# Layer 0 pooling: DMAs from SyncE to ScalarE, and a piece spread over three hooks

## The chip, the cores and the metric

The kernel runs on one core of one Trainium2 chip, in one launch. The metric is the device time of one execution in microseconds; lower is better. TensorE (PE) does the matmuls, VectorE (DVE), ScalarE (ACT) and GpSimd (POOL) the elementwise work, and SyncE (SP) only issues DMAs. ScalarE and GpSimd can issue DMAs too. Each engine works through its own instructions in order.

## The reference

One inference step of a two-layer trunk, for 2048 latent tokens and 128 context tokens (2176 columns, feature width 1024). Layer 0 projects the modulated tokens with one weight into a latent attention part, a pooling input and gates:

```python
q_lat, kv_lat, k_pe, gate_a, pool_in, gate_b = jnp.split(h @ w_in, SPLITS_AB, axis=-1)
o_a = mla_attend(q_nope, q_pe, k_nope, keys_pe, v)
o_b = multiscale_pool(pool_in, w_pool, pool_scale)
mixed = jnp.concatenate([o_a * silu(gate_a), o_b * silu(gate_b)], axis=-1)
return mixed @ w_out
```

The pooling takes four groups of 128 channels with windows w of 2, 4, 8 and 16 tokens. For each token it takes the mean over its window, less the token itself, times a matrix of the group and a scale; the result is multiplied by SiLU of gate_b. Latent and context tokens are pooled apart. Layer 1 is a gated MLP with position mixing; the change doesn't touch it.

## The kernel before

All activations are transposed: 128 channels on the partitions, tokens along the row. The tokens are cut into five blocks of 512, 512, 512, 384 and 256 columns (`BLOCKS`). The pooling matrices are merged into the projection weights beforehand (`merges`, into `wp_d`), so that the projection gives the input of the pooling with the matrix already applied.

Layer 0's input projections run block by block (the loop at L746). In each block `linear` computes pairs of 128 x 512 outputs: one pair each for kv and q, and two pairs each for the pooling input, gate_b and gate_a. A pair is 2 x 8 x 3 = 48 matmuls into one of two PSUM tiles (`psA`); every product is split into a high and a low part, hence three matmuls (`mm3`, L177 to L179). A weight tile of 512 KB is loaded by SyncE into one of four raw tiles (`wload`, L421), cast to the high part by ScalarE (L423), and the low part is formed by VectorE (`sub`, L160). The raw tile is free once both are done. ScalarE evacuates a finished pair (L592) to SBUF, and SyncE stores it to DRAM (`up_d` for the pooling input, `gb_d` and `ga_d` for the gates). In the middle of a block VectorE and ScalarE also normalise kv and q, rotate keys and queries (L492 to L495, L511, L545, L562, L579), and prepare the next block (`prep0`: sums of squares, then `modulate`, L357, L361, L351).

The pooling of a block's tokens is done during the next block, as a generator that is moved on at hooks. A block has eight hooks: one after kv, one after q, and one after each of the six later pairs; each moves the pooling on by one `yield`, and `drain(pools)` at the block's end finishes what is left. Four pieces of tokens (0 to 504, to 1016, to 1528, to 1912) are pooled so, each in four groups. Per group: two loads by SyncE (`up_d` with 8 columns more on each side, and `gb_d`), the window sums on GpSimd (L640, L644, the edges at L634 to L651), the gate on VectorE (L654: mean minus token; L656: scale times gate), and a store by SyncE into `mix_d`. A group takes four tiles of the pool `pl`, which has four. The window sums go back and forth between two of them; the one that holds no result is free when the sums are done, the token tile after L654, the gate tile after L656, the result tile when its store has landed. The next group takes them as they come free.

All DMAs of `store` have line L167 in the profile, whatever they move. The order of the instructions on each engine is not the order of the code. The framework plans it: it goes through the code with its own estimates of durations, takes for each engine what it believes to be ready, and among ready instructions the one that stands first in the code. An instruction may so be put well ahead of its place in the code. On the chip each engine then keeps to that order and waits where an estimate was wrong. DMAs of SyncE and ScalarE take turns on eight semaphores; a DMA also waits until the one before it on its semaphore has landed.

The pooling of the last tokens and of the context comes later, in the attention stage (`last_pooling`, L1257), with tiles of another pool.

Of the kernel before, what the change touches and what calls it, by code (L numbers as in the profile page):

```python
# [50 lines left out]
LD_MIX = 's'  # L51
LD_X = 'a'
LD_PREP = 's'
LD_POOL = 's'
LD_ADA = 's'
LD_GT = 'a'
PRE1 = 1
# [6 lines left out]
AR_POST = 1  # L64
AR_H1 = 0
POOL_AT = 0
POOL_Y = 0
ST_POOL = 's'
ST_EV = 's'
ST_QH = 's'  # L70
ST_QL = 's'
# [42 lines left out]
def trunk_kernel(ctx, tc, xT, cols_in, cond_in, ident_in, edge_in, rope_in, w_ada, w_ada_T, w_in_t, w_inp_T, w_pool,  # L114
# [51 lines left out]
    def store(c, *a):  # L166
        qs[c].dma_start(*a)  # L167
# [36 lines left out]
    up_d = dram.tile([4, P, T], F32, name="up_d")  # L204
    gb_d = dram.tile([4, P, T], F32, name="gb_d")
    ga_d = dram.tile([4, P, T], F32, name="ga_d")
    mix_d = dram.tile([8, P, T], F32, name="mix_d")
# [402 lines left out]
    def pooling(t0, t1, lo_t, hi_t, alloc=pool_tiles, size=PT):  # L610

        m = -(-(t1 - t0) // size)
        cuts = [t0 + (t1 - t0) * i // m for i in range(m + 1)]
        for a, b in zip(cuts[:-1], cuts[1:]):
            yield from pool_piece(a, b, lo_t, hi_t, alloc)

    def pool_piece(t0, t1, lo_t, hi_t, alloc):
        for gi in range(4):
            gate = pool_sums(gi, t0, t1, lo_t, hi_t, alloc)
            yield  # L620
            gate()
            if POOL_Y:
                yield

    def pool_sums(gi, t0, t1, lo_t, hi_t, alloc):

        w = WINDOWS[gi]
        n = t1 - t0
        L = n + 16
        u, gt, cur, other = alloc()  # L630
        a, b = max(t0 - 8, lo_t), min(t1 + 8, hi_t)
        c0 = a - (t0 - 8)
        if c0:
            G.memset(u[:, :c0], 0.0)  # L634
        c1 = c0 + b - a
        if c1 < L:
            G.memset(u[:, c1:L], 0.0)
        store(LD_POOL, u[:, c0:c1], up_d[gi, :, a:b])
        store(LD_POOL, gt[:, :n], gb_d[gi, :, t0:t1])
        G.tensor_tensor(out=cur[:, 1:L], in0=u[:, 0:L - 1], in1=u[:, 1:L], op=ALU.add)  # L640
        a0, a1, step = 1, L, 1
        while 2 * step < w:
            b0, b1 = a0 + step, a1 - step
            G.tensor_tensor(out=other[:, b0:b1], in0=cur[:, b0 - step:b1 - step],  # L644
                            in1=cur[:, b0 + step:b1 + step], op=ALU.add)
            cur, other = other, cur
            a0, a1, step = b0, b1, 2 * step
        if t0 == lo_t:
            G.tensor_tensor(out=cur[:, 8:16], in0=cur[:, 8:16], in1=edge[:, gi, 0:8], op=ALU.mult)
        if t1 == hi_t:  # L650
            G.tensor_tensor(out=cur[:, n:n + 8], in0=cur[:, n:n + 8], in1=edge[:, gi, 8:16], op=ALU.mult)  # L651

        def gate():
            V.scalar_tensor_tensor(out=cur[:, 8:8 + n], in0=cur[:, 8:8 + n], scalar=1.0 / w,  # L654
                                   in1=u[:, 8:8 + n], op0=ALU.mult, op1=ALU.subtract)
            V.scalar_tensor_tensor(out=cur[:, 8:8 + n], in0=cur[:, 8:8 + n],  # L656
                                   scalar=cols[:, C_PS + gi:C_PS + gi + 1],
                                   in1=gt[:, :n], op0=ALU.mult, op1=ALU.mult)
            store(ST_POOL, mix_d[4 + gi, :, t0:t1], cur[:, 8:8 + n])
        return gate  # L660

    def head_loads():
        uq, uk, up = ht(F32, (P, 4, 256)), ht(F32, (P, 4, P)), ht(F32, (P, 2, 2, P))
# [280 lines left out]
    for j in range(16):  # L944
        b = Blk()
# [6 lines left out]
    b = Blk()  # L952
# [304 lines left out]
    def last_pooling():  # L1257
        todo = []
        for t0, t1, lo_t, hi_t in ((BLOCKS[-1][0] - 8, DEC, 0, DEC), (DEC, T, DEC, T)):
            for gi in range(4):  # L1260
                todo.append(pool_sums(gi, t0, t1, lo_t, hi_t, pool_tiles_late))
                if len(todo) > 2:
                    todo.pop(0)()
                yield
        for gate in todo:
            gate()
    pools = last_pooling()
    finishing = []
    g.gated = None
    for i in range(len(steps) + LAG + PV_BEHIND + 2):  # L1270
# [7 lines left out]
        if i < len(steps):  # L1278
            b, p = steps[i]
# [13 lines left out]
        if 0 <= j < len(steps):  # L1293
            b, p = steps[j]
# [134 lines left out]
```

## Time and profile before

| | us |
|---|---|
| median of 3 runs | 2058.27 |
| lowest, highest | 2052.21, 2059.74 |
| profiled execution | 2053.45 |
| its span, first to last instruction | 2051.7 |
| TensorE busy | 1986.3 |
| VectorE busy | 1467.2 |
| ScalarE busy | 1108.1 |
| GpSimd busy | 581.3 |
| mean granted TensorE clock | 0.993 of full speed |

Times in rows are microseconds from the start of the span, unless marked ns. PE is TensorE's matmuls, PEld its weight loads; a letter q behind an engine is its sequencer, which issues DMAs. A row's brackets give the engine's idle time before the instruction and what ended it. The granted clock is the share of full speed that the throttle allowed.

### The profile page before, as it was taken

The numbers are of one execution on the slowest core, as the hardware profiler recorded it, in microseconds if no ns is written. First come the engines' busy times: TensorE is split into PE (matmuls) and PEld (weight loads), VectorE is DVE, ScalarE is ACT, GpSimd is POOL, SyncE is SP. The second block draws the span as 40 slices with busy tenths as digits, with TensorE's granted clock in tenths as the row PEclk, the third lists the DMA queues.
The fourth block names the chain that finished last, engine by engine and source line by source line (L and its number), as shares of the span: only waits on it lengthen the run. The fifth ranks groups of instructions, "written<-read, shape, count | busy, mean of one in ns | idle before, by whom it ended". The sixth has DMA issues, their size and how long they took to land.

```text
span 2051.7 us, 26144 instructions
## 1 busy us (share of the span) xinstructions
PE 1986.3 (97%) x9652; PEld 1661.7 (81%) x9652; DVE 1467.2 (72%) x2222; ACT 1108.1 (54%) x1301; POOL 581.3 (28%) x405
## 2 busy tenths in 40 slices
PE   6999898999999999999999999999999999999997
PEld 3787787998777777777758788888889888889987
DVE  4698887765888888888884997455665566577575
ACT  4644344544676767676754635442454335535554
POOL 1002111111478787878762110001001110010000
PEclk9999999999999999999999999999999999999999
DMA  9587777676111010101135553344434542464463
GB/s 362 186 271 244 259 219 244 193 240 195 51 32 52 27 51 29 49 30 49 36 125 174 184 206 124 123 136 152 164 100 137 184 148 89 134 226 154 131 228 124
DMA packets 123696, 300.62 MB, mean 147 GB/s; under 512 B 12144, under 2 KB 39088, under 8 KB 123568
## 3 DMA queue, kind: packets, MB, share of 16 engines
q1 hardware_dynamic: 105168, 258.58, 38.2%
q10 hardware_dynamic: 13728, 23.60, 3.7%
q0 software_dynamic: 4672, 16.78, 2.3%
q8 instruction: 76, 1.25, 0.3%
q14 instruction: 52, 0.43, 0.1%
HBM read 243.23 MB, written 55.67 MB: 146 GB/s over the span
## 4 chain that ended last, share of the span: by engine, by line
PE 78%; DVE 9%; DMA 4%; issue 3%; ACT 3%; POOL 1%; SPq 1%; DVEq 0%; ACTq 0%; POOLq 0%
PE psA L177 17%; PE psA L178 17%; PE psA L179 17%; PE psA L821 3%; PE psA L822 3%; PE psA L823 3%; PE psA L824 3%; PE psA L825 3%; PE psB L178 2%; PE psB L179 2%; PE psB L177 2%; PE psB L917 2%; DVE w L160 1%; DMA r<-wp_d 1%; PE psB L1173 1%
## 5 line engine op out<-in xcount | busy, mean ns | idle before, releaser
L177 PE MATMUL psA<-h,w 128*128 128x512 f32 (+2 forms) x1600 | 578.3, 362 | 17.8 <-ACT e L592 16.1
L179 PE MATMUL psA<-h,w 128*128 128x512 f32 (+2 forms) x1600 | 574.0, 359 | 0.0
L160 DVE TENSOR_TENSOR w<-r,w 128x1024 fp32r<-128x1024 f32 x280 | 351.8, 1260 | 296.3 <-PE psA L178 199.8
L178 PE MATMUL psA<-h,w 128*128 128x512 f32 (+2 forms) x1536 | 550.0, 358 | 1.1 <-DVE h L160 1.1
L423 ACT CAST w<-r 128x1024 fp32r<-128x1024 f32 x280 | 291.9, 1049 | 253.2 <-PE psA L179 172.8
L177 PEld LDWEIGHTS psA<-h,w 128*128 128x128 f32 x1600 | 303.7, 190 | 58.8 <-ACT e L592 17.9
L179 PEld LDWEIGHTS psA<-h,w 128*128 128x128 f32 x1600 | 303.5, 190 | 38.3 <-issue 0.2
L178 PEld LDWEIGHTS psA<-h,w 128*128 128x128 f32 x1536 | 291.9, 190 | 37.7 <-DVE h L160 2.2
L874 POOL TENSOR_TENSOR w<-h,w 128x1024 fp32r<-128x1024 f32 x105 | 252.4, 2417 | 104.6 <-ACT w L872 101.3
L846 DVE TENSOR_TENSOR run<-psA,run 128x512 f32<-128x512 f32 x240 | 163.8, 683 | 42.1 <-ACT h L836 38.3
L836 ACT COPY h<-psA 128x1024 f32<-128x1024 f32 (+1 forms) x145 | 139.4, 962 | 78.2 <-PE psA L825 78.0
L868 ACT ACTIVATE h<-h 128x1024 f32<-128x1024 f32 (+1 forms) x145 | 143.4, 1011 | 64.0 <-DVE h L866 63.8
L866 DVE TENSOR_TENSOR h<-h,psC 128x1024 f32<-128x1024 f32 (+1 forms) x145 | 163.7, 1147 | 0.7 <-PE psC L860 0.7
L178 PE MATMUL psA<-o,w 128*128 128x512 f32 (+2 forms) x368 | 134.0, 366 | 0.0
L887 POOL TENSOR_TENSOR e<-e,h 128x512 f32<-128x512 f32 x92 | 120.8, 1313 | 5.3 <-ACT h L868 0.5
L872 ACT CAST w<-h 128x1024 fp32r<-128x1024 f32 x105 | 110.5, 1052 | 4.1 <-PE psB L179 3.1
L179 PE MATMUL psA<-o,w 128*128 128x512 f32 (+2 forms) x304 | 109.1, 361 | 0.0
L177 PE MATMUL psA<-o,w 128*128 128x512 f32 (+2 forms) x304 | 108.9, 361 | 0.0
L177 PE MATMUL psA<-w,h 128*128 128x512 f32 x272 | 106.7, 393 | 1.6 <-ACT o L1149 1.6
L640 POOL TENSOR_TENSOR pl<-pl 128x527 f32<-128x527 f32 (+2 forms) x16 | 18.8, 1177 | 308.7 <-DMA pl<-up_d 227.1
L178 PE MATMUL psA<-w,h 128*128 128x512 f32 x272 | 106.0, 390 | 0.1
L179 PE MATMUL psA<-w,h 128*128 128x512 f32 x272 | 105.9, 390 | 0.0
(298 smaller groups left out, 3543.2 us busy)
## 6 DMA issues: line engine op xcount, KB each, us to landing
r<-in_w_inc_t_dram SPq DMA_DIRECT2D x80, 512.0 KB, 3.5
r<-in_w_in_t_dram SPq DMA_DIRECT2D x60, 512.0 KB, 4.3
r<-in_w_oap_t_dram SPq DMA_DIRECT2D x40, 512.0 KB, 3.5
r<-in_w_incv_t_dram SPq DMA_DIRECT2D x40, 512.0 KB, 4.2
r<-in_w_outc_t_dram SPq DMA_DIRECT2D x40, 512.0 KB, 3.4
r<-in_w_ada_T_dram SPq DMA_DIRECT2D x32, 512.0 KB, 4.4
r<-wp_d SPq DMA_DIRECT2D x20, 512.0 KB, 5.6
h<-in_w_ada_dram SPq DMA_DIRECT2D x16, 512.0 KB, 10.2
```

Source lines behind the costliest of these rows:

```text
L160: eng.tensor_tensor(out=out, in0=a, in1=f(hi), op=ALU.subtract)
L177: PE.matmul(ps, w[0], x[0], start=first, stop=False)
L178: PE.matmul(ps, w[0], x[1], start=False, stop=False)
L179: PE.matmul(ps, w[1], x[0], start=False, stop=last)
L423: S.copy(hi, raw)
L836: S.copy(s[:, :nt], ps[:, :nt])
L846: V.tensor_tensor(out=b.max, in0=ps[:, a], in1=s[:, 0] if p == 0 else b.max, op=ALU.max)
L866: V.tensor_tensor(out=s[:, :nt], in0=s[:, :nt], in1=b.m[:, None, :].broadcast_to([P, nt, QB]), op=ALU.subtract)
L868: S.activation(out=s[:, :nt], in_=s[:, :nt], func=AF.Exp, scale=SM_SCALE)
L872: S.copy(ph[:, :nt], s[:, :nt])
L874: low = behind(G.tensor_tensor(out=pl[:, :nt], in0=s[:, :nt], in1=f(ph[:, :nt]), op=ALU.subtract), g.gated)
L887: behind(G.tensor_tensor(out=b.pool[:, 0], in0=b.pool[:, 0], in1=s[:, a], op=ALU.add), low or g.gated)
```

## The change

The loads and the store of a pooling piece are issued by ScalarE in the projection stage (the queue is now an argument, `"a"` there and `"s"` in the attention stage). The store is taken out of `gate` and handed back as a function of its own, which is called one hook later, just ahead of the next group's loads and sums. So a group takes two hooks where it took one: sums at a hook, gate at the next, store (and the next group's sums) at the one after. A piece of four groups had been done at the fifth hook; now it takes all eight hooks of a block, and its last store comes with the `drain` at the block's end. No arithmetic is added or removed, and no bytes. In `last_pooling` gate and store are still called one behind the other.

```diff
-LD_POOL = 's'
-POOL_Y = 0
-ST_POOL = 's'
     def pool_piece(t0, t1, lo_t, hi_t, alloc):
         for gi in range(4):
-            gate = pool_sums(gi, t0, t1, lo_t, hi_t, alloc)
+            gate, out = pool_sums(gi, t0, t1, lo_t, hi_t, alloc, "a")
             yield
             gate()
-            if POOL_Y:
-                yield
-
-    def pool_sums(gi, t0, t1, lo_t, hi_t, alloc):
+            yield
+            out()
+
+    def pool_sums(gi, t0, t1, lo_t, hi_t, alloc, q):
...
-        store(LD_POOL, u[:, c0:c1], up_d[gi, :, a:b])
-        store(LD_POOL, gt[:, :n], gb_d[gi, :, t0:t1])
+        store(q, u[:, c0:c1], up_d[gi, :, a:b])
+        store(q, gt[:, :n], gb_d[gi, :, t0:t1])
...
-            store(ST_POOL, mix_d[4 + gi, :, t0:t1], cur[:, 8:8 + n])
-        return gate
+        return gate, lambda: store(q, mix_d[4 + gi, :, t0:t1], cur[:, 8:8 + n])
...
-                todo.append(pool_sums(gi, t0, t1, lo_t, hi_t, pool_tiles_late))
+                todo.append(pool_sums(gi, t0, t1, lo_t, hi_t, pool_tiles_late, "s"))
                 if len(todo) > 2:
-                    todo.pop(0)()
+                    for it in todo.pop(0):
+                        it()
                 yield
-        for gate in todo:
-            gate()
+        for its in todo:
+            for it in its:
+                it()
```

## Rows read from the trace of the kernel before

**Rows 1.** The page: busy time of each engine, share of the span, instructions.

```profile
PE 1986.3 (97%) x9652; PEld 1661.7 (81%) x9652; DVE 1467.2 (72%) x2222; ACT 1108.1 (54%) x1301; POOL 581.3 (28%) x405
```

**Rows 2.** Sums of the stage: us; PE, PEld, DVE, ACT, POOL; clock, DMA share, GB/s.

```profile
140.00:460.00 320.00, 301.87 (x1456) 262.89 (x1455) 250.82 (x435) 141.12 (x188) 52.60 (x47) 0.97 0.72 233
```

**Rows 3.** Timeline of TensorE, its idle times in that stage: start, us, instruction, idle.

```profile
184.75 0.47 PE L319 MATMUL psD<-e,ones 128*128 128x512 f32 x1 [2.11 <-DVE e L295]
...
218.78 0.80 PE L177 MATMUL psA<-h,w 128*128 128x512 f32 x1 [6.23 <-ACT e L592]
...
324.39 0.79 PE L177 MATMUL psA<-h,w 128*128 128x512 f32 x1 [6.17 <-ACT e L592]
...
414.27 0.68 PE L177 MATMUL psA<-h,w 128*128 128x384 f32 x1 [3.41 <-ACT e L592]
```

**Rows 4.** Sums over 8 us: ahead of the second hole, after the third; columns as before.

```profile
204.00:212.00 8.00, 8.00 (x37) 6.63 (x36) 8.00 (x13) 1.99 (x3) 4.04 (x3) 1.00 0.50 153
...
324.00:332.00 8.00, 7.61 (x24) 6.12 (x25) 5.36 (x13) 3.32 (x5) 0.00 (x0) 0.69 0.95 320
```

**Rows 5.** Timeline of ScalarE ahead of the second and the third hole.

```profile
214.11 1.04 ACT L423 CAST w<-r 128x1024 fp32r<-128x1024 f32 x1 [3.89 <-DMA r<-in_w_in_t_dram]
...
217.70 1.02 ACT L592 ACTIVATE e<-psA 128x1024 f32<-128x1024 f32 x1
...
320.86 1.14 ACT L361 ACTIVATE h<-h,mod 128x384 fp32r<-128x384 f32 x2 [1.58 <-DVE h L357]
```

**Rows 6.** Waits of SyncE's queue, 138 to 460 us: us in total, times, longest.

```profile
SPq L421 <- DVE w L160: 53.9, 26, 7.4
SPq L421 <- DVE psE L266: 20.5, 9, 4.0
SPq L167 <- POOL pl L644: 19.1, 6, 8.4
...
SPq L167 <- DVE pl L656: 17.3, 8, 6.9
...
SPq L167 <- DMA up_d<-e: 9.8, 3, 5.0
...
SPq L167 <- DVE pl L654: 4.9, 6, 2.0
...
SPq L167 <- DMA h<-in_xT_dram: 2.5, 2, 1.5
```

**Rows 7.** Timeline of SyncE ahead of the second and the third hole.

```profile
198.23 0.33 SPq L167 DMA_DIRECT2D mix_d<-pl  x1
...
207.09 0.32 SPq L167 DMA_DIRECT2D pl<-up_d  x1
...
207.98 2.25 SPq L421 DMA_DIRECT2D r<-in_w_in_t_dram  x2
...
308.33 0.32 SPq L167 DMA_DIRECT2D mix_d<-pl  x1
```

**Rows 8.** Instructions on the pooling tiles, 138 to 460 us: ns min/median/max, starts.

```profile
L654 DVE SCALAR_TENSOR_TENSOR pl<-pl,pl x16: 553/669/695, 150.3 to 447.2; 128x512 f32<-128x512 f32 x8, 128x504 f32<-128x504 f32 x4, 128x384 f32<-128x384 f32 x4
L656 DVE SCALAR_TENSOR_TENSOR pl<-pl,cols,pl x16: 612/737/753, 155.4 to 447.8; 128x512 f32<-128x512 f32 x8, 128x504 f32<-128x504 f32 x4, 128x384 f32<-128x384 f32 x4
L167 SPq DMA_DIRECT2D mix_d<-pl x16: 320/326/617, 159.7 to 454.3; - x16
```

**Rows 9.** DMAs of 256 KB that ScalarE issues: ns on its queue, min/median/max.

```profile
L167 ACTq DMA_DIRECT2D e<-ga_d x16: 326/326/354, 554.9 to 1067.5; - x16
```

**Rows 10.** Timeline of VectorE: gates ahead of holes, and the transpose L295.

```profile
183.25 0.72 DVE L656 SCALAR_TENSOR_TENSOR pl<-pl,cols,pl 128x504 f32<-128x504 f32 x1
183.90 0.70 DVE L295 STREAM_TRANSPOSE e<-psD 128x512 f32<-128x512 f32 x1
...
307.55 0.75 DVE L656 SCALAR_TENSOR_TENSOR pl<-pl,cols,pl 128x512 f32<-128x512 f32 x1
```

**Rows 11.** Timeline of SyncE: the first pooling load of all.

```profile
93.72 0.33 SPq L167 DMA_DIRECT2D pl<-gb_d  x1
```

## The prediction

> **What bounds the kernel now.** I read the page first: TensorE is busy for 97% of the span, VectorE for 72%, ScalarE for 54% [rows 1]. So a change pays only where it removes idle time of TensorE, or a fall of its clock. The diff touches the input projections of layer 0, about 140 to 460 us, so the second view is the sums over that stretch: there TensorE is busy 301.9 of 320 us, VectorE 250.8, ScalarE only 141.1, and the mean granted clock is 0.97 [rows 2]. The third view is the timeline of TensorE alone in that stretch. It has four holes, of 2.11, 6.23, 6.17 and 3.41 us, 17.9 us together; the first ended on a VectorE transpose, the others on ScalarE's evacuation L592 of a full PSUM pair [rows 3]. The fourth view, the 8 us windows around them, shows two things [rows 4]. Ahead of the second hole VectorE is full, 8.00 of 8 us. After a hole the granted clock is down, between the levels of 2.4 and 1.2 GHz: 0.69 in the window after the third hole, which costs 0.31 x 8 = 2.5 us. I take 2 us for each hole, an estimate from that one, so 8 in all. What the change can win at most is therefore 17.9 + 8 = 25.9 us, 1.3%.
>
> Why does ScalarE evacuate late? Its own timeline shows it waiting in program order for others [rows 5]: before the second hole a cast waited 3.89 us for a weight tile, and the evacuation stood behind that cast; before the third it waited for VectorE's modulation (L361 behind L357). VectorE's lag and ScalarE's order make the holes, not ScalarE's load.
>
> **The change part by part. (1) SyncE gets free.** Its waits in the stretch are in [rows 6]. Pooling's DMAs wait on it for GpSimd 19.1 us, for the gate's second step (L656) 17.3, for landed stores of up_d 9.8, for the gate's first step 4.9: 51.1 us in which every DMA behind them stands still. That looks like the prize, but the weight loads (L421) wait longer for something else: 53.9 and 20.5 us for VectorE, which has to release one of the four raw tiles. The worst place shows how the two meet [rows 7]. A load of up_d waited for GpSimd up to 207.09, 8.4 us of the first sum. The two weight loads behind it went at 207.98, yet took 2.25 us of queue for two issues, where the load before them took 0.32, because the first still waited inside for VectorE. With the pooling load gone it would have waited for VectorE all the same. I read the other places likewise, and take **0** for this part. Its ends are 0 and the whole 25.9 us, since a load that goes earlier somewhere else I can't exclude.
>
> Nor do I give a gain to a second queue as such: the transfers keep the DMA engines busy for 0.72 of the stretch at 233 GB/s [rows 2], and the change moves the same bytes. The Trainium skill (DMA: Bandwidth & Descriptors, section "Issuing engines are not separate DMA queues") speaks against the change: DMAs from ScalarE and SyncE share the same 16 engines, and a second issuer saves only the time of issuing. By that rule the part is worth the issues alone, and nothing on the path; the waits of 51.1 us are what it leaves out.
>
> **(2) ScalarE issues 48 DMAs** (4 pieces x 4 groups x 3). The nearest row is its own loads of 256 KB: 0.326 us of its queue each [rows 9]; 48 x 0.326 = 15.6 us over 320 us in which it is busy 44%. Ahead of the holes it counts: five pooling DMAs were issued in the 21 us before the end of the second hole and of the third, the first at 198.23, the last at 308.33 [rows 7]. 5 x 0.326 = **+1.6 us**; ends 0 and +15.6. Elsewhere the cover is that ScalarE is idle for more than half of the time; were it gone, the rest of the 15.6 would show.
>
> **(3) The waits move with the DMAs.** What is queued behind a waiting DMA on ScalarE: weight casts, evacuations (L592, L562) and the modulation, for which TensorE and VectorE wait. The third hook puts the store a step after the gate, so the 17.3 us of L656 should be over before the store is issued. Left are 19.1 + 9.8 + 4.9 = 33.8 us. TensorE has a second PSUM pair as cover: 48 matmuls, at 37 in 8 us [rows 4] 10.4 us. The longest wait is 8.4, so in an undisturbed place the cover holds, and I take **0**; ends 0 and +33.8. Only in the stretch ahead of a hole is the cover used up already. The wait for a semaphore slot goes along too: loads stood on SyncE until x tiles which they don't read had landed, 2.5 us in two waits [rows 6]; that is the block's start, where ScalarE waits for weights anyway.
>
> **(4) The gate moves back.** Two VectorE instructions, 0.67 + 0.74 = 1.4 us per group [rows 8], 16 x 1.4 = 22 us in all, none removed. But the hooks of a block lie about a pair apart (10.4 us), and before, a piece used five of the block's eight hooks, from its start; now it uses all eight and the end. So gates leave the first half of a block, where VectorE is full. The gate's second step stood directly ahead of the transpose that ended the first hole (183.25 before 183.90), and another, at 307.55, in the run-up to the third [rows 10]. One pair of gate instructions before each of the first three holes: 3 x 1.4 = **-4.2 us**. Ends: 0 (no gate moves) and -4.2 - 3 x 2 (the clock with them) = -10.2.
>
> **(5) The rest.** The last store of a piece now comes at the end of its block. Before, the last of all was issued at 454.3 us, at the start of the last block [rows 8]; the next user of these tiles waits for it, and the sums of a piece are needed only in the output projection. 0; ends 0 and 5.0 us, the longest that SyncE waited for a landed store [rows 6]. In the pooling of the attention stage gate and store still follow each other on SyncE: 0.
>
> **Sum** against the profiled execution of 2053.45 us (span 2051.7, and 1.75 around it): 0 + 1.6 + 0 - 4.2 + 0 = -2.6, so 2050.85. The median of the three runs, 2058.27, lies 4.82 above that execution, and what is compared is a median: 2050.85 + 4.82 = **2055.7 us**.
>
> **The rivals. A, the forecast:** holes shrink a little, the issues take a little back: 2055.7.
> **B, faster:** the weight loads did stand behind the pooling loads, and with SyncE free VectorE runs ahead of TensorE. Then the second and third hole go with their clock, and the first shrinks by a gate: 6.23 + 6.17 + 2 x 2 + 1.4 = 17.8, so 2058.3 - 17.8 = 2040.5. For it: the 8.4 us ahead of two weight loads, and the cast that then waited 3.89 us for weights [rows 5, 7]. Against: 74 us of VectorE waits in the same queue [rows 6].
> **C, slower:** a pooling load stands on ScalarE ahead of an evacuation in a full stretch and waits for GpSimd or for a store of up_d. It decides from the point where the second PSUM pair is full, that is, where the wait and ScalarE's lateness together pass 10.4 us; ahead of the second and third hole they already do. Price: 8.4 + 5.0 (the longest waits for GpSimd and for up_d [rows 6]; the first of them ended at 207.09, ahead of the second hole [rows 7]) + 2 x 2 for the clock + 1.6 = 19.0, so 2077.3. For it: three of the four holes already end on ScalarE [rows 3]. Against: the store no longer follows the gate at once, and ScalarE is idle for half of the stretch. The Trainium skill (PSUM — Partial Sum Buffer, section "Engine vs sequencer instructions") has the rule by which this goes: ScalarE's queue is strictly first in, first out. The trace agrees, as the evacuation at 217.70 behind the cast of 214.11 shows.
> **D, the hooks do little:** the planner puts a pooling DMA where its own estimate has the inputs ready, whatever the hook. The first load of gb_d was issued at 93.72 us, 57 us ahead of the first gate [rows 8, 11]. Then the gates stay where they are and only the issues move: +1.6, 2059.9.
>
> **How the numbers follow.** A 0.36, D 0.15, B 0.27, C 0.22. 0.5% is 10 us, about what a measurement of this kernel can tell from no change. A and D lie within it, B is below and C above: faster 0.27, same 0.51, slower 0.22. The bounds of B are 2032 (all 25.9 us) to 2048; C begins at 2069. The range 2037 to 2075 leaves out about 0.08 of B and 0.10 of C.
>
> **What would show it.** SyncE's waits for GpSimd and L656 must be gone (1). ScalarE must show 48 issues of about 0.33 us in the stretch (2); waits of several us in front of them, with L592 or a cast behind, show C (3). The gates' starts should lie in the second half of a block, and the first hole be under 1 us (4). TensorE's holes are the judge: near 15 us in four for A, 6 or less for B, over 30 for C. I am wrong most easily if the planner, given other queues, orders the whole stage anew, so that holes appear at places that none of these steps names.

## The result and the profile of the changed kernel

The changed kernel takes 2071.07 us (median of 6 runs, 2068.64 to 2074.73), the kernel before 2059.01 (6 runs, 2052.21 to 2061.73). The ratio is 1.0064, 95% interval 1.0048 to 1.0081: slower by 12.1 us. The profiled executions lie 17.3 us apart (2070.78 against 2053.45), because the one of before was 5.6 us under its median; of a delay read from the two traces, some 5 us are therefore not the change's.

The page and the sums over the stage, with columns as in [rows 1, 2]; the second row of sums is the stretch where most is lost:

```profile
PE 1991.6 (96%) x9652; PEld 1663.4 (80%) x9652; DVE 1461.7 (71%) x2222; ACT 1109.3 (54%) x1301; POOL 578.7 (28%) x405
...
140.00:460.00 320.00, 292.91 (x1360) 250.28 (x1359) 237.51 (x430) 135.83 (x178) 49.89 (x47) 0.97 0.68 225
160.00:190.00 30.00, 20.86 (x83) 15.81 (x82) 13.52 (x19) 8.03 (x9) 9.97 (x12) 0.87 0.68 235
```

From 140 to 460 us TensorE is busy 9.0 us less than before (292.91 for 301.87), VectorE 13.3 and ScalarE 5.3 less, at the same mean clock. No engine has more to do; they stand. The 30 us from 160 on are the worst. The kernel before, over the same 30 us:

```profile
160.00:190.00 30.00, 27.89 (x116) 22.58 (x115) 25.18 (x44) 17.63 (x20) 7.04 (x7) 0.94 0.80 275
```

TensorE is busy 7.0 us less there, VectorE 11.7 and ScalarE 9.6. TensorE's idle times of over 1 us in the stage of the changed kernel, from its timeline (start, us, instruction, idle before it):

```profile
180.39 0.49 PE L316 MATMUL psD<-e,ones 128*128 128x512 f32 x1 [3.61 <-ACT e L286]
182.29 0.80 PE L317 MATMUL psD<-e,ones 128*128 128x512 f32 x1 [1.40 <-DVE e L157]
184.31 0.80 PE L174 MATMUL psA<-h,w 128*128 128x512 f32 x1 [1.23 <-ACT w L420]
188.42 0.79 PE L176 MATMUL psA<-h,w 128*128 128x512 f32 x1 [2.89 <-DVE w L157]
...
230.63 0.50 PE L174 MATMUL psA<-h,w 128*128 128x512 f32 x1 [2.42 <-ACT e L589]
...
338.76 0.67 PE L174 MATMUL psA<-h,w 128*128 128x512 f32 x1 [4.83 <-ACT e L589]
...
429.29 0.45 PE L174 MATMUL psA<-h,w 128*128 128x384 f32 x1 [3.15 <-ACT e L589]
```

Lines are three lower than in the kernel before as far as the pooling (L592 is now L589, L160 is L157, L644 is L641, L654 is L651). With four more of 1 to 2.7 us they make 26.4 us, against 17.9 in four [rows 3]. The three that ended on the evacuation L592 shrank, from 6.23, 6.17 and 3.41 to 2.42, 4.83 and 3.15; new is the cluster from 180 to 190.

What ScalarE waited for on pooling's account, 90 to 475 us (us in total, times, longest); in the kernel before this view has no such row:

```profile
ACT w L420 <- DMA pl<-gb_d: 9.3, 1, 9.3
ACT w L420 <- POOL pl L641: 8.3, 1, 8.3
ACT e L589 <- POOL pl L641: 8.0, 1, 8.0
ACT e L286 <- POOL pl L631: 6.8, 1, 6.8
...
ACT e L545 <- DMA gb_d<-e: 3.7, 1, 3.7
...
ACT e L589 <- DVE pl L653: 2.3, 1, 2.3
```

With three shorter ones they come to 41.9 us. VectorE's waits at the gates and for landing stores of `gb_d` rose as well, from 16.8 to 50.3 us. The waits of both, added up in this way, are given with each experiment below. The sums go by the name that the view gives, and so leave out one long wait of ScalarE: 13.63 us in front of the kv evacuation L501, shown next. With it the 41.9 are 55.5.

How the cluster comes about is read from three timelines, one after the other. ScalarE (ACTq is a DMA issue on its queue):

```profile
160.62 0.33 ACTq L164 DMA_DIRECT2D mix_d<-pl  x1
169.21 0.33 ACTq L164 DMA_DIRECT2D pl<-up_d  x1
170.21 0.33 ACTq L164 DMA_DIRECT2D pl<-gb_d  x1
171.04 0.33 ACTq L164 DMA_DIRECT2D mix_d<-pl  x1
171.41 1.02 ACT L501 COPY e<-psA 128x1024 f32<-128x1024 f32 x1 [13.63 <-DMA r<-wp_d]
172.32 0.60 ACT L503 ACTIVATE e<-psA 128x512 f32<-128x512 f32 x1
179.27 0.33 ACTq L164 DMA_DIRECT2D pl<-up_d  x1
179.72 0.62 ACT L286 CAST e<-e 128x512 fp32r<-128x512 f32 x1 [6.80 <-POOL pl L631]
```

GpSimd:

```profile
168.13 1.05 POOL L641 TENSOR_TENSOR pl<-pl 128x517 f32<-128x517 f32 x1 [5.53 <-DMA mix_d<-pl]
...
175.83 1.05 POOL L637 TENSOR_TENSOR pl<-pl 128x519 f32<-128x519 f32 x1 [6.33 <-DMA pl<-up_d]
177.07 2.17 POOL L641 TENSOR_TENSOR pl<-pl 128x517 f32<-128x517 f32 x2 [0.19 <-DMA mix_d<-pl]
```

VectorE:

```profile
169.49 0.68 DVE L651 SCALAR_TENSOR_TENSOR pl<-pl,pl 128x504 f32<-128x504 f32 x1 [7.81 <-POOL pl L631]
...
179.56 0.68 DVE L651 SCALAR_TENSOR_TENSOR pl<-pl,pl 128x504 f32<-128x504 f32 x1 [8.61 <-POOL pl L631]
180.28 0.74 DVE L653 SCALAR_TENSOR_TENSOR pl<-pl,cols,pl 128x504 f32<-128x504 f32 x1
```

The store of the first group went at 160.62, and GpSimd could go on behind its landing only at 168.13: it left at the start of the second block, among loads of x, weights and the rope table. GpSimd needed its tile for the second group and waited 5.53 us. VectorE stood at the second group's gate meanwhile (7.81), ScalarE at the next load of up_d (up to 169.21), since the third group's tile comes free only when the second group's sums are done. Then the same once more for the third group: the load issued at 169.21 let GpSimd go on at 175.83, VectorE stood for 8.61 us, ScalarE until 179.27. The kv evacuation L501, for which the view names a weight load, really stood behind the three issues from 169.21 on: it ran at 171.41, in the kernel before at 160.39. From 160 to 180 us ScalarE did two evacuations, and VectorE one cast, one gate and the beginning of the next, so casts, the next block's squares and evacuations were late, and TensorE idled.

In the kernel before the chain was slower: its DMAs stood in SyncE's order among the others, and the second and third group's gates ran at 180.92 and 196.31 us, without a wait of VectorE:

```profile
180.92 0.67 DVE L654 SCALAR_TENSOR_TENSOR pl<-pl,pl 128x504 f32<-128x504 f32 x1
...
196.31 0.61 DVE L654 SCALAR_TENSOR_TENSOR pl<-pl,pl 128x504 f32<-128x504 f32 x1
```

A second, smaller place lies earlier. The first load of gb_d, which SyncE issued at 93.72 [rows 11], now stands on ScalarE and waits there for the store of gb_d that it reads:

```profile
96.73 0.35 ACTq L164 DMA_DIRECT2D pl<-gb_d  x1
97.21 1.05 ACT L545 CAST e<-e 128x1024 fp32r<-128x1024 f32 x1 [3.71 <-DMA gb_d<-e]
...
109.54 1.03 ACT L589 ACTIVATE e<-psA 128x1024 f32<-128x1024 f32 x1
```

The evacuation at 109.54 ran at 103.24 in the kernel before.

### The profile page after: what moved, and what is told of

It is laid out like the page before. It is cut to its first block, busy times and chain, and to the rows that moved or that the text cites. A ratio compares the mean times of both kernels' runs of the same rounds, so it can differ in the third digit from the quotient of the medians.

```text
span 2069.0 us, 26138 instructions
## 1 busy us (share of the span) xinstructions
PE 1991.6 (96%) x9652; PEld 1663.4 (80%) x9652; DVE 1461.7 (71%) x2222; ACT 1109.3 (54%) x1301; POOL 578.7 (28%) x405
## 4 chain that ended last, share of the span: by engine, by line
PE 72%; DVE 7%; DMA 2%; ACT 2%; issue 2%; POOL 1%; SPq 0%; ACTq 0%; DVEq 0%; POOLq 0%
PE psA L174 15%; PE psA L175 15%; PE psA L176 15%; PE psA L817 3%; PE psA L818 3%; PE psA L819 3%; PE psA L820 3%; PE psA L821 3%; PE psB L175 2%; PE psB L176 2%; PE psB L174 2%; PE psB L913 2%; DVE w L157 1%; PE psE L1169 1%; DMA r<-wp_d 1%
## 5 line engine op out<-in xcount | busy, mean ns | idle before, releaser
L157 DVE TENSOR_TENSOR w<-r,w 128x1024 fp32r<-128x1024 f32 x280 | 351.0, 1257 | 290.7 <-PE psA L175 198.4
```

The lines of the kernel that those rows point to most:

```text
L157: eng.tensor_tensor(out=out, in0=a, in1=f(hi), op=ALU.subtract)
```

## The experiments

Ratios are to the kernel before on the same chip, with their 95% intervals; the waits are the sums named above, ScalarE / VectorE (before: 0 / 16.8 us; changed: 41.9 / 50.3). For the long wait of the kv evacuation at about 170 us the view of e1 names the gate, and its 13.9 us are counted; in the changed kernel (13.6) and in e9 (13.9) it names a weight load, and they are not. Counted alike these two have 55.5 and 28.8 us of ScalarE.

| kernel | ratio | waits, us |
|---|---|---|
| changed | 1.0064 [1.0048, 1.0081] | 41.9 / 50.3 |
| e1 queue alone | 1.0069 [1.0045, 1.0093] | 51.8 / 46.9 |
| e2 hooks alone | 0.9991 [0.9977, 1.0006] | 3.2 / 22.2 |
| e3 only loads on ScalarE | 1.0026 [1.0015, 1.0038] | 37.2 / 29.3 |
| e4 only stores on ScalarE | 1.0016 [1.0006, 1.0026] | 23.1 / 28.0 |
| e5 48 issues that wait for nothing | 1.0007 [0.9996, 1.0018] | 0 / 19.7 |
| e6 all on GpSimd | 1.0105 [1.0090, 1.0120] | 0 / 65.9 |
| e8 first piece on SyncE, rest on ScalarE | 1.0029 [1.0013, 1.0045] | 35.1 / 41.0 |
| e9 first piece on ScalarE, rest on SyncE | 1.0080 [1.0061, 1.0098] | 14.9 / 40.3 |
| e10 changed, gates held at their hooks | 1.0106 [1.0087, 1.0125] | 36.2 / 3.4 |
| e11 changed, DMAs held at their hooks | 1.0001 [0.9989, 1.0012] | 1.2 / 14.5 |
| e12 e6 with gates held | 1.0031 [1.0017, 1.0045] | 0 / 4.3 |
| e13 changed, both held | 1.0015 [1.0004, 1.0027] | 3.4 / 7.8 |
| e14 e11, last piece on SyncE | 1.0003 [0.9988, 1.0018] | 2.8 / 15.1 |
| e15 e9 with its DMAs held | 0.9980 [0.9968, 0.9991] | 0 / 29.8 |

**The two halves of the change, e1 and e2.** e1 is the kernel before with the queue alone changed; e2 is the changed kernel with SyncE as the queue.

```diff
 # e1, against the kernel before
-LD_POOL = 's'
+LD_POOL = 'a'
-ST_POOL = 's'
+ST_POOL = 'a'
 # e2, against the changed kernel
-            gate, out = pool_sums(gi, t0, t1, lo_t, hi_t, alloc, "a")
+            gate, out = pool_sums(gi, t0, t1, lo_t, hi_t, alloc, "s")
```

> The kernel before, with the loads and stores of a piece issued by ScalarE in the projection stage, and hooks as before (gate and store at one hook). Theory W (ScalarE stands at pooling's DMAs until GpSimd, VectorE or a landed store lets them go, and casts and evacuations stand behind): as slow as the change or slower, since the store again follows its gate at once, ratio 1.006 to 1.012. Theory H (the loss comes from the later hooks, which make the planner order VectorE and ScalarE anew): no change, 0.998 to 1.002. Theory I (the 48 issues of 0.33 us on ScalarE alone): 1.004 to 1.008, and no waits of several us before the issues.

> The changed kernel with the pooling's DMAs back on SyncE: only the hooks differ from before. Theory W: the loss is gone, ratio 0.996 to 1.002. Theory H: the loss stays, 1.005 to 1.008. Theory I: the loss is gone, as in W.

The queue alone gives the whole loss, the hooks alone nothing that can be measured. So the theory of later hooks falls. The gain of 4.2 us that I had given them, a ratio of 0.998, isn't shown either, though it lies just inside e2's interval.

**Loads or stores alone, e3 and e4.** The same kernel, with `pool_sums` taking one queue for its loads and one for its store.

```diff
 # e3
+            gate, out = pool_sums(gi, t0, t1, lo_t, hi_t, alloc, "a", "s")
 # e4
+            gate, out = pool_sums(gi, t0, t1, lo_t, hi_t, alloc, "s", "a")
```

> The changed kernel with the loads on ScalarE and the stores on SyncE. Theory W: the loads carry the long waits (for GpSimd's sums, for landed stores of up_d and gb_d), so most of the loss stays, 1.004 to 1.008. Theory I: two thirds of the loss, 1.004. Theory H: 1.006, as the change.

> The changed kernel with the loads on SyncE and the stores on ScalarE. Theory W: stores wait for the gate's second step only, a hook later, so little is lost, 1.000 to 1.003. Theory I: one third of the loss, 1.002. Theory H: 1.006.

Measured from e2, which has the same hooks and no pooling DMA on ScalarE, the loads cost 0.35% and the stores 0.25%; both together cost 0.73%. Within the intervals the two parts add up. The length of ScalarE's waits doesn't set the price: e3 has 37.2 us of them for 0.26%, e9 below 28.8 us, counted alike, for 0.80%. In e3 and e4, with one kind of DMA left on SyncE, the second group's gate comes at 186.2 and 187.0 us, not at 169.49 as in the changed kernel.

**The issues alone, e5.** The kernel before, with 48 stores of 4 KB more on ScalarE, one at each of 48 weight casts, of data that is long ready, into a scratch tensor that nobody reads.

```diff
         S.copy(hi, raw)
+        casts.append(hi)
+        n = len(casts) - 13
+        if 0 <= n < 48:
+            nc.scalar.dma_start(probe[n], f(casts[-2]).rearrange("p a b -> p (a b)")[:, :8])
```

> The kernel before, with 48 more DMAs issued by ScalarE in the projection stage, one behind a weight cast each, from the fourteenth tile on. Each stores 8 columns of the weight tile cast one step before into an unused DRAM tensor, so that it waits for nothing that is late: ScalarE pays the issue and no wait. Theory I (the issues make the loss): 1.004 to 1.008. Theory W (the waits in front of the issues make it): 0.998 to 1.003, an upper bound, since these DMAs come on top and take semaphore slots of their own.

1.0007, and 1 lies in its interval, which is -0.8 to 3.7 us: my +1.6 us for the issues fits, the 15.6 us of their sum are excluded. The Trainium skill (DMA: Bandwidth & Descriptors, section "Issuing engines are not separate DMA queues") calls the time of issuing small beside the DMA; this run agrees, with 0.33 us for an issue and a median of 3.2 us to its landing. But the time of issuing is not all that a queue decides: e1, with 48 issues too, costs 0.69%.

**A third queue, e6.** All pooling DMAs and the hooks of the change on GpSimd.

```diff
-            gate, out = pool_sums(gi, t0, t1, lo_t, hi_t, alloc, "a")
+            gate, out = pool_sums(gi, t0, t1, lo_t, hi_t, alloc, "g")
```

> The changed kernel with the same DMAs and the same hooks issued by GpSimd, which makes the sums and has nothing else to do in that stage. Theory W: the waits stay, but nobody stands behind them, so 0.994 to 1.002. Theory Q (a queue beside SyncE's takes bandwidth from the weight loads, whoever issues): as slow as the change, 1.005 or more.

This missed. ScalarE has no pooling wait left and the loss is larger, 1.0105. VectorE's timeline shows the same two waits as in the changed kernel, 5 us earlier:

```profile
164.74 0.69 DVE L651 SCALAR_TENSOR_TENSOR pl<-pl,pl 128x504 f32<-128x504 f32 x1 [7.71 <-POOL pl L631]
...
174.91 0.68 DVE L651 SCALAR_TENSOR_TENSOR pl<-pl,pl 128x504 f32<-128x504 f32 x1 [8.70 <-POOL pl L631]
```

So ScalarE's waits can't be the whole theory. What e1, e6 and the changed kernel share is that the chain of a piece is no longer behind SyncE's other DMAs, and that the planner puts its gates earlier. VectorE's order shows it. Ahead of the second and third group's gates it has formed, from the start of the execution, the low parts of 23 and 26 weight tiles in the kernel before, and of 24 and 29 in e2, e3, e4 and e8, where at least one kind of the first piece's DMAs is on SyncE. In the changed kernel, e1, e6 and e9, where none is, it is 20 and 20, and there VectorE stands 7.7 to 8.8 us at each of the two gates.

**Which piece, e8 and e9.**

```diff
 # e8
+            gate, out = pool_sums(gi, t0, t1, lo_t, hi_t, alloc, "a" if t0 else "s")
 # e9
+            gate, out = pool_sums(gi, t0, t1, lo_t, hi_t, alloc, "s" if t0 else "a")
```

> The changed kernel with the first piece's 12 DMAs back on SyncE, the other 36 on ScalarE. In the trace of the change most of the loss is there by 200 us, that is, in the first piece. Theory W, place by place: the early part goes, about 1.002 to 1.004 stays. Theory I: three quarters of the loss, 1.005.

> The changed kernel with only the first piece's 12 DMAs on ScalarE, the other 36 on SyncE. Theory W, place by place: the larger part of the loss, 1.003 to 1.007. Theory I: a quarter of the loss, 1.0015.

The 12 DMAs of the first piece lose as much as all 48, with 28.8 us of waits on ScalarE, counted alike, while the other 36 come to 1.0029 with 35.1. So neither the number of DMAs nor the length of the waits decides, but the place. The first piece is pooled in the second block, and its first store goes out while the DMA engines are busy (0.90 from 160 to 168 us, last section); whether that load is needed for the loss was not tested apart from the order.

**Holding the steps at their hooks, e10 to e13.** The planner may put an instruction ahead of its place in the code. Here it is tied, for order only, behind the last VectorE cast (gates) or the last ScalarE evacuation (DMAs) that the code has issued before it. In these kernels the evacuation is L591.

```diff
 # e10 and e12: the gate's first step
+            if alloc is pool_tiles:
+                behind(ins, g.last_v)
 # e11: loads and store
+                behind(ins, g.last_s)
 # e13: both; e12: e6 with the gates held
```

> The changed kernel, with one thing added: in the projection stage the first instruction of each gate is ordered behind the VectorE cast that was issued last at its hook, so that the gate stays where its hook is and VectorE doesn't take it earlier. Queues as in the change. Theory W2 (the pooling chain is placed early, at the loaded start of a block, and the engines that stand in order at its steps, VectorE at the gate and ScalarE at the DMAs, are late with casts and evacuations): VectorE's waits for pooling tiles fall from 50 us to under 20, the wait of some 8 us at 169 us is gone, ratio to the kernel before 0.997 to 1.003. Rival S (ScalarE's own waits at the DMAs make the loss, VectorE's are a consequence): the ratio stays at 1.005 to 1.009.

> The changed kernel, with one thing added: in the projection stage each pooling DMA on ScalarE is ordered behind the evacuation that was issued last at its hook; the gates are free. Theory W2: the chain can't start early, so that both ScalarE's waits (42 us) and VectorE's (50 us) fall to under 20 us each, and the ratio to the kernel before is 0.997 to 1.003. Rival S expects the same of ScalarE and of the ratio, but VectorE's waits unchanged or higher. Rival Q (a second queue on the loaded DMA engines): unchanged, 1.005 to 1.009.

> The kernel of the GpSimd queue (all pooling DMAs issued by GpSimd, ratio 1.0105) with the gates ordered behind the cast that was issued last at their hooks. Theory W2: there VectorE alone stood at the gates, 65.9 us; this falls to under 20, and the ratio to 0.997 to 1.003. Rival G (DMAs issued by GpSimd cost by themselves: late landings, late sums): the ratio stays at 1.007 or above, with VectorE's waits gone.

> The changed kernel with both held at their hooks: each pooling DMA behind the last evacuation on ScalarE, each gate behind the last cast on VectorE. That is the change as my forecast took it, gates out of a block's first half and no wait of ScalarE. Theory W2: waits of both engines for pooling tiles under 15 us each, ratio 0.994 to 1.000. Rivals S and Q as above: S 0.997 to 1.003, Q 1.005 to 1.009.

e10 missed, and it says most. VectorE's waits are gone, 3.4 us, the first cluster too (TensorE is busy for all of 160 to 190 us); but the loss is 1.0106. With the gates late, ScalarE's loads wait for later sums, now ahead of full PSUM pairs; its timeline:

```profile
437.52 1.05 ACT L422 CAST w<-r 128x1024 fp32r<-128x1024 f32 x1 [3.36 <-PE psA L178]
445.88 0.33 ACTq L166 DMA_DIRECT2D pl<-up_d  x1
446.33 0.81 ACT L591 ACTIVATE e<-psA 128x768 f32<-128x768 f32 x1 [7.75 <-POOL pl L643]
```

and TensorE, behind it:

```profile
447.19 0.69 PE L176 MATMUL psA<-h,w 128*128 128x384 f32 x1 [3.46 <-ACT e L591]
```

That is rival C, to the letter: a load of up_d waits for GpSimd, an evacuation stands behind it, TensorE waits for the evacuation. So on ScalarE's queue its own waits suffice for the loss, and VectorE's are not needed (rival S of that expectation): e13, which is e10 with these DMAs held too, comes to 1.0015. On GpSimd's queue, where ScalarE has no pooling wait, holding the gates takes two thirds of the loss away (e12: 1.0031 for 1.0105; just above the range I gave). What is left there lies in the three holes on the evacuation, 8.30, 9.72 and 4.70 us, 22.7 for 15.8 before [rows 3]; its cause stays open. So either engine's waits alone can make the loss, ScalarE's in e10 and VectorE's in e6; how the changed kernel's loss divides between them isn't shown. e11 holds only ScalarE's DMAs: both engines' waits fall, and the loss is gone, with the 48 DMAs still on ScalarE. That excludes the queue as such. Its sums, columns as before:

```profile
140.00:460.00 320.00, 304.79 (x1484) 266.35 (x1483) 248.09 (x440) 145.22 (x194) 41.91 (x38) 0.97 0.70 230
160.00:190.00 30.00, 30.00 (x134) 24.68 (x133) 22.68 (x45) 17.31 (x20) 0.00 (x0) 1.00 0.73 249
```

TensorE is 2.9 us busier in the stage than before the change, and yet the kernel isn't faster. The lead goes at the end of the stage, at the last piece, on ScalarE and then TensorE:

```profile
501.06 0.38 ACTq L166 DMA_DIRECT2D mix_d<-pl  x1
501.49 1.01 ACT L839 COPY h<-psA 128x1024 f32<-128x1024 f32 x1 [3.55 <-DVE pl L656]
...
504.57 0.80 PE L824 MATMUL psA<-r,K 128*128 128x512 f32 x1 [4.02 <-DVE run L849]
```

The store is not the whole cause of this hole. The run step L849 on VectorE, which released TensorE, stood behind a gate of the last pooling that waited for GpSimd; the kernel before has a hole of 1.70 us at that place:

```profile
503.61 0.30 DVE L654 SCALAR_TENSOR_TENSOR e<-e 128x136 f32<-128x136 f32 x1 [2.63 <-POOL e L651]
```

e13 was to be the change as I had forecast it: gates where the hooks are, no waits of ScalarE. It came out at 1.0015, not at 0.999. TensorE's hole at 184 us is gone, but three are left where there were three, and one is new:

```profile
213.69 0.79 PE L176 MATMUL psA<-h,w 128*128 128x512 f32 x1 [5.66 <-ACT e L591]
288.05 0.47 PE L318 MATMUL psD<-e,ones 128*128 128x512 f32 x1 [1.19 <-DVE e L294]
321.66 0.80 PE L176 MATMUL psA<-h,w 128*128 128x512 f32 x1 [7.57 <-ACT e L591]
412.52 0.69 PE L176 MATMUL psA<-h,w 128*128 128x384 f32 x1 [5.28 <-ACT e L591]
```

19.7 us, against 17.9 before [rows 3]. The gates are later, but they aren't away from the holes. Held behind the last cast, two of a piece's four gates stand in the run-up to each of the three large ones; ahead of the first of these:

```profile
192.35 0.67 DVE L654 SCALAR_TENSOR_TENSOR pl<-pl,pl 128x504 f32<-128x504 f32 x1
...
199.26 0.69 DVE L654 SCALAR_TENSOR_TENSOR pl<-pl,pl 128x504 f32<-128x504 f32 x1 [1.20 <-POOL pl L633]
```

The others start at 298.16 and 305.60, and at 394.33 and 401.30. In the 25 us ahead of the same three holes the kernel before has two gates, one and none. So e13 isn't a test of gates that have left the run-up.

**Two repairs, e14 and e15.** e14 is e11 with the last piece on SyncE; e15 is e9, the run in which 12 DMAs lost everything, with those 12 held as in e11.

```diff
 # e14
+            gate, out = pool_sums(gi, t0, t1, lo_t, hi_t, alloc, "s" if t0 > 1500 else "a")
 # e15
+            gate, out = pool_sums(gi, t0, t1, lo_t, hi_t, alloc, "s" if t0 else "a")
```

> The changed kernel with each pooling DMA ordered behind the last evacuation of its hook, as in the run that came out at 1.0001, but the DMAs of the last piece (12 of 48) issued by SyncE. In that run ScalarE's evacuations were 2 to 5 us earlier than in the kernel before from 387 to 469 us, and then ScalarE stood at the last piece's store (3.55 us) and TensorE idled 4.02 us at 504.57 us, at the start of the attention stage. If the lead is given back there: that hole under 1.5 us, ratio 0.997 to 0.9995. If the lead is only the run's own difference: ratio 0.9995 to 1.0015.

> Only the first piece's 12 DMAs on ScalarE, as in the run that lost most (1.0080), but each ordered behind the last evacuation of its hook; the other 36 on SyncE. If the place of these 12 DMAs in ScalarE's order makes the loss: ratio 0.997 to 1.0015, VectorE's waits of 8.1 and 8.6 us at 168 and 178 us gone, TensorE without a hole of over 1 us from 160 to 190 us. If it is the queue (bytes, issues, where the landing is reported) whatever the place: 1.005 to 1.008.

e15 decides its question: 0.9980 instead of 1.0080, with the same queue, bytes and issues; the order alone moved. It is also the fastest of all, 2055.67 us against 2058.66, a gain of 3 us. That the gain comes from these 12 DMAs isn't shown: e2, with the same hooks and all of them on SyncE, has 0.9991, and the two intervals overlap. In e15's timeline TensorE has no hole over 1 us from 160 to 190, and the first two gates of the first piece stand at 157.45 and 200.23 without a wait, the second behind 26 weight tiles where e9 has 20:

```profile
157.45 0.69 DVE L654 SCALAR_TENSOR_TENSOR pl<-pl,pl 128x504 f32<-128x504 f32 x1
...
200.23 0.67 DVE L654 SCALAR_TENSOR_TENSOR pl<-pl,pl 128x504 f32<-128x504 f32 x1
```

e14 decides nothing: the hole at the start of the attention stage shrank from 4.02 to 1.85 us, but another opened before it, where VectorE had stood 4.5 us at a gate of the last piece, and 1.0003 fits both expectations.

## Why the prediction was wrong, step by step

The forecast was 2055.7 us, a little faster; measured were 2071.07, within the range of 2037 to 2075 but on the other side. Rival C was right in kind.

**What bounds the kernel** holds: TensorE's holes are the judge, and the holes follow ScalarE's and VectorE's order, not their load. The sum of the holes grew by 8.5 us in the stage, and TensorE's busy time there fell by 9.0.

**(1), SyncE gets free: 0.** It fits. Pooling's waits for GpSimd and for the gate are gone from SyncE, and the weight loads wait as they did, only longer, from 53.9 and 20.5 us [rows 6] to:

```profile
SPq L418 <- DVE w L157: 71.4, 24, 8.1
...
SPq L418 <- DVE psE L263: 30.8, 8, 9.8
...
SPq L164 <- DMA pl<-up_d: 6.3, 1, 6.3
```

That speaks against rival B: the weight loads wait for VectorE, whatever else is in the queue. The last row is something that I had not foreseen. SyncE still waits for landings of pooling DMAs, 11.6 us in all, though ScalarE issues them. The 6.3 us are a load of `in_w_ada_T` that went at 175.73: its turn on the eight semaphores came behind ScalarE's load of up_d, which it doesn't read. In e6 SyncE has no such wait and the loss is larger, so the loss doesn't need it.

**(2), the issues: +1.6.** e5 fits it.

**(3), the waits move to ScalarE: 0, ends 0 and +33.8.** This is the step that failed. Even the upper end was too low for the waits themselves, 41.9 us or, with the kv evacuation's, 55.5, since I took SyncE's waits as they stood in a chain that SyncE itself slowed. The cover was mis-argued in two ways. I compared each wait with the 10.4 us of the second PSUM pair one by one; but the waits of one chain follow each other (a store's landing, then a load's), with issues between them, and from 160 to 180 us hardly anything else got through on ScalarE. And I looked only at ScalarE: the same chain also holds VectorE at its gates (50.3 us), so both engines that feed TensorE were late at once. The place was another too: not ahead of the second and third hole, but at the start of the second block, where I had written that ScalarE waits for weights anyway.

**(4), the gates leave the first half of a block: -4.2.** Wrong as well. In the changed kernel they didn't leave it: the second and third group's gates came at 169.49 and 179.56, before the change at 180.92 and 196.31. The hook sets only the place in the code; the planner, which had the chain's DMAs off SyncE, put the gates ahead. That is what rival D said of the DMAs; I hadn't applied it to the gates. What a gate ahead of a hole costs stays open. In e13 the first hole went, as I had written. The other three made 18.5 us for 15.8, but with six gates in the 25 us ahead of them where the kernel before has three. In the changed kernel no gate starts in these stretches, and the three holes make 10.4 us. That is the direction of the term, but the changed kernel had lost time ahead of these places, and no run moves the gates and leaves the rest as it was.

**(5), the rest: 0.** It fits the change, whose last store was issued at 457.8 us. In e11, where the last piece runs up to 501 us, TensorE idles 4.02 us where it idled 1.70 before, in part behind that piece's store.

**Rival C** gave 2077.3, 6 us too much, from four prices that were not those of the actual places; its point of decision, a second PSUM pair that is full, is what e10 shows at 447 us. The sign that I had set for it, holes of over 30 us, was not reached: they make 26.4. As the sentence at the end had it, I was wrong where the planner, given other queues, ordered the stage anew.

## What to carry to other kernels

A DMA that must wait holds up what stands behind it in its queue; moving it frees one engine's order and loads another's, and the issue itself is the least of it. An idle engine's queue isn't enough, as e6 shows: the order of a third engine moved with it. Where a planner orders instructions by estimates, a chain that was slowed by a busy queue is pulled forward when it leaves that queue, into the place where its transfers land late; before forecasting a gain, follow every engine that takes part in the chain, and add up waits that follow each other before comparing them with a buffer. If the DMAs are to move, tie them to the place where their inputs are surely there: the kernel with the same 12 DMAs on ScalarE came out at 1.0080 untied and at 0.9980 tied.

## What the runs showed of the hardware

The store of 252 KB that was issued at 160.62 us was waited for until 168.13, 7.5 us. In that time the DMA engines were busy for 0.90 and moved 302 GB/s, and ScalarE computed nothing (columns as in [rows 2]):

```profile
160.00:168.00 8.00, 8.00 (x37) 6.60 (x36) 1.68 (x2) 0.00 (x0) 1.91 (x1) 1.00 0.90 302
```

The median from issue to landing of all pooling DMAs in the stage was 3.9 us. 48 DMAs more on ScalarE, with nothing to wait for, cost between -0.04% and 0.18%; the same number with pooling's waits (e1) 0.45% to 0.93%. GpSimd as the queue was no better than ScalarE, 1.0105, although it left ScalarE without a pooling wait; an issue took 0.55 us of GpSimd, 0.33 of ScalarE.
